# Decoder layer: a late head-norm part is chained behind the one before it, and the additions to finished tiles are spread over eight steps of one down-projection stage

## The chip, the core and the metric

The kernel is one program on one core of a Trainium2 chip. The core has five engines that run side by side, each with its own queue of instructions in a fixed order: TensorE (PE, matmuls), VectorE (DVE), ScalarE (ACT), GpSimd (POOL), and SyncE (SP), which here only issues DMAs. An instruction waits in its queue until the semaphores it names are reached; everything behind it on that engine waits with it. The metric is the time of one execution in microseconds (us), and the median over several is compared.

## What is computed

One layer of a hybrid decoder on 1024 tokens of width 1024, in float32:

```python
h = rms_norm(x, norm1_g);  proj = h @ w_in
y_a = rwkv7_branch(...)          # 8 heads x 64, a recurrence over time
y_b = stick_breaking_branch(...) # causal attention, 8 heads x 64
y_m = memory_branch(...)         # cross attention to 256 memory tokens
x = x + sum_b(sigmoid(G_b) * (y_b @ w_branch[b])) @ w_out
x = x + conv_ffn(x)              # up, causal conv of width 3, SwiGLU, down
# at the end of rwkv7_branch, for each token and head:
y = (y - mean(y)) * rsqrt(var(y) + 64e-5) * lnx_g + lnx_b   # then + bonus, * gate
```

## The kernel before

Every large matmul is done as three products of a high and a low half (`xhi`, `xlo`, `wh`, `wl` and the like): ScalarE copies the high half (L83), POOL subtracts to get the low half (L89), and both come from a weight tile that SP loaded.

**The recurrence** (`stage2`) runs over 16 chunks of 64 tokens, `c` = 0 to 15. A chunk has three parts, each ended by a `yield`: small matmuls into four PSUM tiles `g` and four VectorE copies (L656); matmuls with the inverse and ScalarE copies (L664); then matmuls for state and output, VectorE's state update (L674) and ScalarE's copies of the output into `self.y[p]` (L676), where p = 0 to 3 are pairs of heads. Between the parts, `weave` lets a list of filler items advance: gate items (`gate_item`: a projection in two PSUM tiles `mm`, ScalarE copies L885, a VectorE product with the row norms L886, ScalarE L889) and branch items (`branch_item`: a product in two tiles `mm` that VectorE multiplies by the gate, L1297, and adds, L1299). PSUM holds four tiles of tag `mm`; each item takes two, so the second item after an item takes its two back.

**The head norm** (`norm_part(g0, g1)`) works on output groups g0 to g1 - 1, of two chunks each. It is a generator: VectorE sums per head (L699) and one scaling (L700); ScalarE squares with a running sum (L706), four at a step; VectorE prepares (L192) and POOL takes the power (L195); two or three empty steps; then VectorE scales the heads (L715) in two steps. `stage2` advances it by one step after each `yield`. The parts are (0, 2), (2, 4), (4, 6), (6, 7) and (7, 8), started after chunks 3, 7, 11, 13 and 15. After the last chunk three more steps are taken, and `group_norm` takes the rest while it turns the heads by transposes (L122), multiplies by the gain (L729), adds (L730), and splits into high (L734) and low (L735) halves. `branch_last` then multiplies those by the last branch's weights: the gate of each output tile (L1354), the sum of the branches (L1359), high and low copies (L1365, L1366).

**Order.** Instructions passed through `pinned` keep the order in which the program emits them on their engine; in `stage2` and `group_norm` (`strict`) each is also tied behind the one pinned before. The rest (such as L89, L195, L729, L885) is placed by a list scheduler.

**The down projection** (`down_phase`) has seven stages i = 1, 3, 6, 5, 7, 4, 2 of 11 steps f = 0 to 10. A step is 12 matmuls. `prep`, three steps ahead, loads an activation block and a weight block (L1843, L1846), forms the weight of stages 4 and 7 on VectorE (L1848), makes high halves on ScalarE (L1853, L1854) and low ones on VectorE (L1855) and POOL (L1856). `drain` at f = 10 empties the PSUM tiles and lists finished output tiles in `sums`, with the residual tile `x` that SP loads and the terms to add. In the next stage `complete(tt)` does the additions of tile tt at step tt (L1876), and `release` at f = 5 issues the stores on ScalarE's queue (L1873). After stage 7 there are two terms, `q` and `U`, so in stage 4 two additions a step. At step 9 of stage 4 `last_residual` reloads `q` (L1917) and adds it to `p1` (L1918).

Of the kernel before, what the change touches and what calls it, by code (L numbers as in the profile page):

```python
# [50 lines left out]
class Trunk:  # L51
# [549 lines left out]
    def stage2(self):  # L601
        nc = self.nc
        self.y = [self.t4("qk") for _ in range(4)]
        uv = self.t4("ys", n=512).rearrange("p (u c) -> p u c", u=8)
        U, v1s = [uv[:, p] for p in range(4)], [uv[:, 4 + p] for p in range(4)]
        nc.gpsimd.memset(uv[:, 0:4], 0.0)
        hq = [slice(0, 64), slice(64, 128)]
        heads = [(p, h2) for p in range(4) for h2 in range(2)]
        A, Y, W, S = (slice(o, o + 64) for o in range(0, 256, 64))
        Ls, VTs = {}, {}  # L610
        norm = iter(())

        def load(g, p, what="LV"):
            if "L" in what:
                last = (g * 4 + p) % 8 == 7
                Ls[g, p] = self.t4("it", n=1080)[:, :1024] if last else self.t4("at")
                nc.sync.dma_start(Ls[g, p], self.scr[p, g])
            if "V" in what and p % 2 == 0:
                V2 = self.t4("qk")
                for h2 in range(2):  # L620
                    nc.sync.dma_start(V2[hq[h2], h2 * 256 : h2 * 256 + 256], self.vd[p // 2, h2, g].rearrange("s c i -> s (c i)"))
                nc.sync.dma_start(V2[:, 512:768], self.td[p // 2, g].rearrange("h s p i -> (h s) (p i)"))
                for i in range(2):
                    VTs[g, p + i] = [V2[:, h2 * 256 + i * 128 : h2 * 256 + i * 128 + 128] for h2 in range(2)], V2[:, 512 + i * 128 : 640 + i * 128]

        for p in range(4):
            load(0, p, "L")
        yield
        for p in range(0, 4, 2):
            load(0, p, "V")  # L630
        yield
        for p in range(4):
            load(1, p)
        yield
        for c in range(NC):
            g, cc = c // 2, c % 2
            us = []
            for p in range(4):
                L, (V, TT) = Ls[g, p], VTs[g, p]
                us.append((  # L640
                    U[p], L[:, cc * 128 : (cc + 1) * 128], L[:, 256 + cc * 128 : 256 + (cc + 1) * 128],
                    L[:, 512 + cc * 256 : 512 + (cc + 1) * 256], [v[:, cc * 64 : (cc + 1) * 64] for v in V],
                    TT[:, cc * 64 : (cc + 1) * 64], v1s[p], self.ps("g")))

            def state(o, rs):
                for p, h2 in heads if c else ():
                    Up, ra, _, _, _, _, _, pb = us[p]
                    q = hq[h2]
                    self.mmul(pb[q, o], ra[q, rs], Up[q], start=True, stop=False)

            state(A, Y)
            for p, h2 in heads:
                _, _, _, M, wv, _, v1, pb = us[p]
                self.mmul(pb[hq[h2], A], M[hq[h2], h2 * 128 + 64 : h2 * 128 + 128], wv[h2][hq[h2]], start=(c == 0), stop=True)
                if h2 == 1:
                    self.pinned(nc.vector.tensor_copy(v1, pb[:, A]))  # L656
            yield
            next(norm, None)
            for p, h2 in heads:
                _, _, _, _, wv, tt, v1, pb = us[p]  # L660
                self.mmul(pb[hq[1 - h2], W], tt[hq[h2]], v1[hq[h2]], start=True, stop=True)
                if h2 == 1:
                    for q, w in zip(hq, wv[::-1]):
                        self.pinned(nc.scalar.activation(w[q], pb[q, W], AF.Copy))  # L664
            yield
            next(norm, None)
            state(Y, A)
            for p, (Up, ra, bt, M, wv, tt, v1, pb) in enumerate(us):
                for h2, q in enumerate(hq):
                    self.mmul(pb[q, Y], M[:, h2 * 128 : h2 * 128 + 64], wv[h2], start=(c == 0), stop=True)  # L670
                if c < NC - 1:
                    for h2, q in enumerate(hq):
                        self.mmul(pb[q, S], bt[:, q], wv[h2], start=True, stop=True)
                    self.pinned(nc.vector.scalar_tensor_tensor(Up, Up, self.pc[p][:, c : c + 1], pb[:, S], ALU.mult, ALU.add))  # L674
                for h2, q in enumerate(hq):
                    self.pinned(nc.scalar.activation(self.y[p][cc * 64 : cc * 64 + 64, g * 128 + h2 * 64 : g * 128 + h2 * 64 + 64], pb[q, Y], AF.Copy))  # L676
            if cc and g + 2 < NG:
                for p in range(4):
                    load(g + 2, p)
            yield  # L680
            next(norm, None)
            if c in (3, 7, 11, 13, 15):
                for _ in norm:
                    pass
                norm = self.norm_part(*{3: (0, 2), 7: (2, 4), 11: (4, 6), 13: (6, 7), 15: (7, 8)}[c])
                next(norm)
            if c == 13:
                self.gs = [self.load_gg(p) for p in range(2)]
        for _ in range(3):
            next(norm)  # L690
        self.norm = norm
# [1124 lines left out]
    def down_phase(self):  # L1816
# [58 lines left out]
        puts, sums = [], []  # L1875
        add = lambda o, a, b, op=ALU.add: self.pinned(nc.vector.tensor_tensor(o, a, b, op))  # L1876

        def complete(tt):
            for half, n, x, terms in sums:
                for y in terms:  # L1880
                    add(x[tt], x[tt], y[tt])
                puts.append((half, n, tt, x[tt]))
            if tt == 3:
                sums.clear()

        def release():
            for args in puts:
                put(*args)
            puts.clear()
# [36 lines left out]
        for s, (i, f) in enumerate(steps):  # L1926
# [10 lines left out]
                t_sums(s // 2)  # L1937
            if s + ahead < len(steps):
                prep(s + ahead)
            if f < 4:  # L1940
                complete(f)
            elif f == 5:
                release()
            if s in (2, 4):
                self.last_sums.pop(0)()
# [184 lines left out]
```

## Time and profile before

| | |
|---|---|
| median of 3 runs | 1786.35 us (1785.88 to 1787.78) |
| profiled execution, its own time | 1786.78 us |
| its span, first to last instruction | 1785.0 us |
| recurrence, chunk 13 to the last output copy of chunk 15 | about 942 to 983 us of the span |
| `group_norm` | about 983 to 1011 us |
| `branch_last` | from 1011.6 us |
| down phase, stage 4 | about 1720 to 1750 us |

A row of the profile gives start and length in us, the engine, the line of the kernel, the operation, the tiles (out<-in, numbers left out), shapes and count, and in brackets how long the engine had been idle before it and what ended that. PE rows overlap a little: a matmul of 512 columns follows the one before by 0.23 us.

### The profile page before, as it was taken

How to read it: one execution, taken by the hardware profiler on the slowest of the kernel's cores; microseconds unless marked ns; L12 is line 12 of the kernel's file. 1: busy time of each engine (PE TensorE's matmuls, PEld its weight loads, DVE VectorE, ACT ScalarE, POOL GpSimd, SP SyncE). 2: the span in 40 equal slices, each digit the busy share in tenths (PEclk: the TensorE clock that was granted, in tenths of full speed). 3: DMA queues.
4: the chain of work that ended last, by engine and by line, in shares of the span. 5: the costliest groups of instructions: out<-in, count | busy, mean ns of one | idle time of the engine just before them, and what ended most of it. 6: DMA issues, size and time to landing. Idle time of an engine off the chain costs nothing.

```text
span 1785.0 us, 27451 instructions
## 1 busy us (share of the span) xinstructions
PE 1775.7 (99%) x10481; PEld 1442.9 (81%) x10481; DVE 1184.1 (66%) x1687; ACT 882.8 (49%) x1667; POOL 697.1 (39%) x409
## 2 busy tenths in 40 slices
PE   9999999999999999999999999999999999999999
PEld 7777778878888888787777888888888888888887
DVE  5666674787888655243533882697767777795596
ACT  6543344466566635444556434454444445444343
POOL 1232252322221012022333322257777677545454
PEclk9999999999999999999999999999999999999999
DMA  4256574111112343658764662323323333396475
GB/s 185 72 167 188 180 247 152 51 56 43 54 57 69 111 126 93 201 181 280 264 229 146 236 210 98 115 89 124 101 89 110 109 109 113 109 330 219 142 248 200
DMA packets 120758, 263.39 MB, mean 148 GB/s; under 512 B 28330, under 2 KB 41130, under 8 KB 120499
## 3 DMA queue, kind: packets, MB, share of 16 engines
q1 hardware_dynamic: 82434, 193.31, 32.9%
q10 hardware_dynamic: 34416, 55.72, 8.5%
q0 software_dynamic: 3776, 12.62, 2.4%
q8 instruction: 82, 1.34, 0.3%
q14 instruction: 50, 0.40, 0.1%
HBM read 180.04 MB, written 81.53 MB: 147 GB/s over the span
## 4 chain that ended last, share of the span: by engine, by line
PE 62%; issue 1%; POOL 1%; ACT 1%; DVE 1%; DMA 0%; ACTq 0%; DVEq 0%; POOLq 0%; SPq 0%
PE mm L139 53%; PE g L139 8%; PE g L122 1%; POOL dw L1856 1%; DVE qk L715 0%; ACT wh L83 0%; DMA qk<-vd 0%; ACT w L885 0%; DVE w L886 0%; DVE keep L1876 0%; POOL l L1555 0%; ACT qk L664 0%; ACT ys L1020 0%; DVE wl L86 0%; ACT qk L1059 0%
## 5 line engine op out<-in xcount | busy, mean ns | idle before, releaser
L89 POOL TENSOR_TENSOR wl<-wr,wh 128x1024 fp32r<-128x1024 f32 x58 | 148.0, 2552 | 368.2 <-ACT wh L83 360.5
L139 PE MATMUL mm<-xhi,wh 128*128 128x512 f32 x784 | 260.6, 413 | 0.5 <-ACT w L936 0.4
L139 PE MATMUL mm<-xlo,wh 128*128 128x512 f32 x784 | 243.5, 392 | 0.7 <-DVE xlo L225 0.6
L139 PE MATMUL mm<-xhi,wl 128*128 128x512 f32 x784 | 242.2, 390 | 0.0
L139 PEld LDWEIGHTS mm<-xlo,wh 128*128 128x128 f32 x784 | 147.0, 188 | 34.0 <-DVE xlo L225 1.6
L139 PEld LDWEIGHTS mm<-xhi,wl 128*128 128x128 f32 x784 | 147.1, 188 | 32.6
L139 PEld LDWEIGHTS mm<-xhi,wh 128*128 128x128 f32 x784 | 136.5, 189 | 30.4 <-issue 7.9
L139 PE MATMUL mm<-dw,da 128*128 128x512 f32 x528 | 121.1, 390 | 0.0
L83 ACT ACTIVATE wh<-wr 128x1024 fp32r<-128x1024 f32 x75 | 79.5, 1060 | 81.0 <-PE mm L139 61.9
L139 PE MATMUL mm<-BT,l 128*128 128x512 f32 x504 | 118.0, 389 | 0.3 <-POOL l L1555 0.3
L139 PEld LDWEIGHTS mm<-dw,da 128*128 128x128 f32 x528 | 98.9, 188 | 21.7 <-DVE da L1855 1.2
L1856 POOL TENSOR_TENSOR dw<-draw,dw 128x512 fp32r<-128x512 f32 x55 | 83.1, 1520 | 77.0 <-ACT dw L1854 74.2
L985 DVE TENSOR_TENSOR_SCAN at<-at,at 128x128 f32<-128x128 f32 (+3 forms) x64 | 91.0, 1429 | 33.1 <-ACT at L979 33.0
L139 PEld LDWEIGHTS mm<-BT,l 128*128 128x128 f32 x504 | 94.5, 188 | 20.3 <-POOL l L1555 0.7
L139 PE MATMUL mm<-BT,wh 128*128 128x512 f32 x352 | 108.5, 389 | 0.1
L139 PE MATMUL mm<-B,wh 128*128 128x512 f32 x352 | 108.4, 389 | 0.0
L195 POOL TENSOR_TENSOR hf<-rs,half 128x16 f32<-128x16 f32 (+1 forms) x18 | 49.2, 2732 | 143.4 <-DVE rs L192 138.9
L1855 DVE TENSOR_TENSOR da<-draw,da 128x512 fp32r<-128x512 f32 x77 | 66.6, 873 | 49.0 <-ACT da L1853 48.6
L139 PE MATMUL g<-dw,da 128*128 128x512 f32 x396 | 90.5, 389 | 0.4 <-POOL dw L1856 0.4
L1853 ACT ACTIVATE da<-draw 128x512 fp32r<-128x512 f32 x77 | 48.3, 628 | 81.0 <-PE mm L139 31.7
L139 PEld LDWEIGHTS g<-dw,da 128*128 128x128 f32 x396 | 74.2, 188 | 16.2 <-POOL dw L1856 0.8
L1627 ACT ACTIVATE g<-u,params 128x512 f32<-128x512 f32 x88 | 65.2, 770 | 32.1 <-DVE u L1717 22.9
(345 smaller groups left out, 3956.6 us busy)
## 6 DMA issues: line engine op xcount, KB each, us to landing
wr<-in_w_in_dram SPq DMA_DIRECT2D x49, 512.0 KB, 3.8
draw<-actd SPq DMA_DIRECT2D x77, 256.0 KB, 3.1
at<-scr SPq DMA_DIRECT2D x28, 512.0 KB, 5.5
draw<-in_w_down_dram SPq DMA_DIRECT2D x55, 256.0 KB, 4.6
rw<-in_w_up_dram SPq DMA_DIRECT2D x22, 512.0 KB, 3.5
actd<-gall ACTq DMA_DIRECT2D x41, 256.0 KB, 3.1
gsd<-w ACTq DMA_DIRECT2D x20, 512.0 KB, 2.8
wr<-in_w_up_dram SPq DMA_DIRECT2D x18, 512.0 KB, 3.6
```

The lines of the kernel that those rows point to most:

```text
L83: ins = self.nc.scalar.activation(hi, raw, AF.Copy)
L89: self.last_wl = self.nc.gpsimd.tensor_tensor(lo, raw, hi.bitcast(F32), ALU.subtract)
L122: self.pinned(self.nc.tensor.transpose(out, in_, self.ident[:n, :n]))
L139: self.pinned(self.nc.tensor.matmul(*a, **k))
L195: nc.gpsimd.tensor_tensor(out, t[:, :n], self.half[:, :n], ALU.pow)
L985: self.pinned(nc.vector.tensor_tensor_scan(sn[:, :W][:, ::-1], sn[:, :W][:, ::-1], self.smask[:, 1024 - W :][:, ::-1], 1.0, ALU.mult, ALU. ...
L1627: keep(nc.scalar.activation(c, u[:, 2 + h * 512 : 514 + h * 512], AF.Identity, scale=self.par("cw2", m), bias=self.par("cb", m)))
L1853: self.pinned(nc.scalar.activation(A[:, 0], a, AF.Copy))
L1855: self.pinned(nc.vector.tensor_tensor(A[:, 1], a, A[:, 0].bitcast(F32), ALU.subtract))
L1856: nc.gpsimd.tensor_tensor(Wt[:, 1], w, Wt[:, 0].bitcast(F32), ALU.subtract)
```

## The change

Two edits, with no instruction added or removed.

In `stage2`, after chunk 13 the part (4, 6) is no longer run to its end there, and the part (6, 7) no longer starts there. The two are joined by `itertools.chain`, so (6, 7) starts when (4, 6) has been stepped to its end; what is left after chunk 15 is run through before (7, 8) starts.

In `down_phase`, in stage 4, `complete` takes one term a step over steps 0 to 7 instead of two a step over steps 0 to 3, and the stores are released at step 8 instead of step 5.

```diff
             next(norm, None)
-            if c in (3, 7, 11, 13, 15):
+            if c in (3, 7, 11, 15):
                 for _ in norm:
                     pass
-                norm = self.norm_part(*{3: (0, 2), 7: (2, 4), 11: (4, 6), 13: (6, 7), 15: (7, 8)}[c])
+                norm = self.norm_part(*{3: (0, 2), 7: (2, 4), 11: (4, 6), 15: (7, 8)}[c])
                 next(norm)
+            elif c == 13:
+                norm = itertools.chain(norm, self.norm_part(6, 7))
...
-        def complete(tt):
+        def complete(tt, part=None):
             for half, n, x, terms in sums:
-                for y in terms:
-                    add(x[tt], x[tt], y[tt])
-                puts.append((half, n, tt, x[tt]))
-            if tt == 3:
+                for j, y in enumerate(terms):
+                    if part in (None, j):
+                        add(x[tt], x[tt], y[tt])
+                if part != 0:
+                    puts.append((half, n, tt, x[tt]))
+            if tt == 3 and part != 0:
                 sums.clear()
...
-            if f < 4:
+            if i == 4 and f < 8:
+                complete(f // 2, f % 2)
+            elif i != 4 and f < 4:
                 complete(f)
-            elif f == 5:
+            elif f == (8 if i == 4 else 5):
                 release()
```

The new lines shift the numbers of later lines by two in the changed program: L699 becomes L701, L715 L717, L1297 L1299, and so on to L1876, which becomes L1878.

PE's order is the same in both programs. VectorE, at the end of the recurrence, before: `hn` and `hf` with 9071 and 9222 belong to the part (6, 7), those with 9353 and 9376 to (7, 8); `qk` 6786 to 6789 are the four output tiles; `w_1528` is the gate of a branch item.

```order
L886 TENSOR_TENSOR w_1528_9314<-w_1528_9314,rbc 128x1024
L715 TENSOR_SCALAR qk_6786<-qk_6786,hn_9071,hf_9222 128x64 x2
L715 TENSOR_SCALAR qk_6787<-qk_6787,hn_9071,hf_9222 128x64 x2
L715 TENSOR_SCALAR qk_6788<-qk_6788,hn_9071,hf_9222 128x64 x2
L715 TENSOR_SCALAR qk_6789<-qk_6789,hn_9071,hf_9222 128x64 x2
L699 TENSOR_REDUCE hn_9353<-qk_6786 128x2
L699 TENSOR_REDUCE hn_9353<-qk_6787 128x2
L699 TENSOR_REDUCE hn_9353<-qk_6788 128x2
L699 TENSOR_REDUCE hn_9353<-qk_6789 128x2
L700 TENSOR_SCALAR hn_9353<-hn_9353 128x8
L729 TENSOR_TENSOR at_9078<-g_9402,at_9078 128x512
L729 TENSOR_TENSOR at_9082<-g_9409,at_9082 128x512
```

The same place in the changed program, where (6, 7) has `hn` 9263 and 9264 and `hf` 9341, and the gate is `w_1518`:

```order
L888 TENSOR_TENSOR w_1518_9294<-w_1518_9294,rbc 128x1024
L731 TENSOR_TENSOR at_9055<-g_9402,at_9055 128x512
L731 TENSOR_TENSOR at_9059<-g_9409,at_9059 128x512
L192 TENSOR_SCALAR rs_9342<-hn_9264 128x8
L717 TENSOR_SCALAR qk_6786<-qk_6786,hn_9263,hf_9341 128x64 x2
L717 TENSOR_SCALAR qk_6787<-qk_6787,hn_9263,hf_9341 128x64 x2
L717 TENSOR_SCALAR qk_6788<-qk_6788,hn_9263,hf_9341 128x64 x2
L717 TENSOR_SCALAR qk_6789<-qk_6789,hn_9263,hf_9341 128x64 x2
L701 TENSOR_REDUCE hn_9353<-qk_6786 128x2
L701 TENSOR_REDUCE hn_9353<-qk_6787 128x2
L701 TENSOR_REDUCE hn_9353<-qk_6788 128x2
L701 TENSOR_REDUCE hn_9353<-qk_6789 128x2
```

The preparation of (6, 7), L192, which stood in chunk 14, now stands here, with the wait for POOL's power behind it. In both programs L192 of (7, 8), two L730, four scalings and the branch item's two products (L1297, now L1299) follow; the four L729 that stood between and behind them now all stand ahead of that L192. On POOL the power of (6, 7) stood ahead of two weight splits L89, and now stands behind them.

ScalarE at the same place, before, behind the last gate copy L889:

```order
L889 ACTIVATE w_1528_9314<-w_1528_9314 128x1024
L706 ACTIVATE jk_9360,hn_9354<-qk_6786,hn_9353 128x64
L706 ACTIVATE jk_9362,hn_9354<-qk_6786,hn_9353 128x64
L83 ACTIVATE wh_9426<-wr_9424 128x1024
L706 ACTIVATE jk_9364,hn_9354<-qk_6787,hn_9353 128x64
```

and now:

```order
L891 ACTIVATE w_1518_9294<-w_1518_9294 128x1024
L708 ACTIVATE jk_9325,hn_9264<-qk_6786,hn_9263 128x64
L708 ACTIVATE jk_9327,hn_9264<-qk_6786,hn_9263 128x64
L708 ACTIVATE jk_9329,hn_9264<-qk_6787,hn_9263 128x64
L708 ACTIVATE jk_9331,hn_9264<-qk_6787,hn_9263 128x64
L708 ACTIVATE jk_9333,hn_9264<-qk_6788,hn_9263 128x64
L708 ACTIVATE jk_9335,hn_9264<-qk_6788,hn_9263 128x64
L83 ACTIVATE wh_9426<-wr_9424 128x1024
L708 ACTIVATE jk_9337,hn_9264<-qk_6789,hn_9263 128x64
L708 ACTIVATE jk_9339,hn_9264<-qk_6789,hn_9263 128x64
L708 ACTIVATE jk_9360,hn_9354<-qk_6786,hn_9353 128x64
```

Eight squares of (6, 7) stand where those of (7, 8) began, and the weight copy L83 stands behind six of them instead of two.

ScalarE in `branch_last`, before; `mg` are copies of output tiles (9624 the first, 9634 the second), and `wh_9817` is the high half of the branch weight that the fifth output tile uses, with low half `wl_9818`:

```order
L1365 ACTIVATE mg_0_1_0_9618<-at_9624 128x256
L83 ACTIVATE at_9799<-wr_9801 128x1024
L83 ACTIVATE wh_9817<-wr_9815 128x1024
L1365 ACTIVATE mg_0_0_9608<-at_9634 128x512
L1365 ACTIVATE mg_0_0_0_9616<-at_9634 128x256
L1365 ACTIVATE mg_0_1_0_9618<-at_9634 128x256
```

and now:

```order
L83 ACTIVATE qk_9753<-wr_9755 128x1024
L1367 ACTIVATE mg_0_0_9608<-at_9634 128x512
L1367 ACTIVATE mg_0_0_0_9616<-at_9634 128x256
L1367 ACTIVATE mg_0_1_0_9618<-at_9634 128x256
L83 ACTIVATE at_9799<-wr_9801 128x1024
L83 ACTIVATE wh_9817<-wr_9815 128x1024
```

Both weight copies moved from ahead of the second tile's three copies to behind them.

## The prediction

> **What bounds the kernel now.** I read the page's engine rows first, then the chain that ended last, then PE's waits.
>
> ```profile
> PE 1775.7 (99%) x10481; PEld 1442.9 (81%) x10481; DVE 1184.1 (66%) x1687; ACT 882.8 (49%) x1667; POOL 697.1 (39%) x409
> PE 62%; issue 1%; POOL 1%; ACT 1%; DVE 1%; DMA 0%; ACTq 0%; DVEq 0%; POOLq 0%; SPq 0%
> PE g L139 <- DVE ys L656: 0.5, 1, 0.5
> PE g L139 <- POOL dw L1856: 0.4, 1, 0.4
> ```
>
> TensorE is busy for 99% of the span and heads the chain; all waits that the view puts down to its matmuls add up to 5.0 us (1.5 + 0.6 + 0.6 + 0.5 + 0.5 + 0.4 + 0.4 + 0.3 + 0.2). So an edit that leaves the matmuls alone can gain little, and any new wait of PE is paid in full. The two waits quoted lie where the two edits are. The timeline shows both, with VectorE's work ahead of the first:
>
> ```profile
> 958.66 3.65 DVE L715 TENSOR_SCALAR qk<-qk,hn,hf 128x64 f32<-128x64 f32 x16
> 962.23 0.86 DVE L699 TENSOR_REDUCE hn<-qk 128x2 f32<-128x128 f32 x4
> 963.48 0.72 PE L139 MATMUL g<-ys,qk 64*64 64x64 f32 x16 [0.46 <-DVE ys L656]
> 1740.08 10.95 PE L139 MATMUL g<-dw,da 128*128 128x512 f32 x47 [0.36 <-POOL dw L1856]
> ```
>
> **What the edits remove.** At the end of chunk 13 VectorE did 16 scalings and 4 sums in one block, 4.4 us, ahead of the copy that chunk 14's matmul needed. The block goes: PE gains 0.46. In the down phase one addition a step in place of two lets the weight splits start earlier; the 0.36 may go. Together 0.82 us, and no other wait of PE stands near either edit.
>
> **What the first edit moves.** The part (6, 7) took its 8 squares and its power during chunk 14. Now they stand behind chunk 15, so two norm parts, each sums, squares, power, scalings, follow one another at the end, and the pinned order holds VectorE in that row. What stands behind them there:
>
> ```profile
> 983.67 1.06 ACT L889 ACTIVATE w<-w 128x1024 f32<-128x1024 f32 x1 [0.57 <-DVE w L886]
> 986.50 0.35 ACT L706 ACTIVATE jk<-qk,hn 128x64 f32<-128x64 f32 x1 [1.77 <-DVE hn L700]
> 986.98 0.35 ACT L706 ACTIVATE jk<-qk,hn 128x64 f32<-128x64 f32 x1
> 987.33 1.04 ACT L83 ACTIVATE wh<-wr 128x1024 fp32r<-128x1024 f32 x1
> 988.45 2.38 POOL L89 TENSOR_TENSOR wl<-wr,wh 128x1024 fp32r<-128x1024 f32 x1 [5.89 <-ACT wh L83]
> 969.33 1.67 POOL L195 TENSOR_TENSOR hf<-rs,half 128x8 f32<-128x8 f32 x1 [0.89 <-DVE rs L192]
> 991.35 2.01 POOL L195 TENSOR_TENSOR hf<-rs,half 128x8 f32<-128x8 f32 x1 [0.52 <-DVE rs L192]
> 983.56 1.87 DVE L715 TENSOR_SCALAR qk<-qk,hn,hf 128x64 f32<-128x64 f32 x8
> 986.24 0.17 DVE L700 TENSOR_SCALAR hn<-hn 128x8 f32<-128x8 f32 x1
> 993.40 0.98 DVE L715 TENSOR_SCALAR qk<-qk,hn,hf 128x64 f32<-128x64 f32 x4 [0.92 <-POOL hf L195]
> 994.29 1.28 DVE L1297 TENSOR_TENSOR w<-mm,w 128x512 f32<-128x512 f32 x2
> 998.81 0.61 PE L139 MATMUL mm<-xhi,wh 128*128 128x512 f32 x2
> ```
>
> The last two rows are the place that decides. L1297 empties the two `mm` banks of the last branch item. There are four such banks, each item takes two, one gate item follows, and the second gate item, which starts at 998.81, takes those two back. L1297's halves end at about 994.95 and at 995.57, so the first bank has 3.8 us in hand.
>
> Now the new row, on the trace's clock. ScalarE is done with L889 at 984.73. Six squares at 0.48 (986.98 less 986.50): 987.61. L83 1.04: 988.65. Two squares: 989.6. VectorE's 0.17: 989.8. POOL's split of that weight runs 988.7 to 991.1 and stands ahead of the power, so the power of (6, 7) (1.67) ends at 992.8, and VectorE waits 3 us for it. Eight scalings, four sums and L700 took 983.56 to 986.41, 2.85, and one PSUM product L729 of 0.65 now stands among them: 996.3. Eight squares of (7, 8) at 0.48: 1000.2. L192 and the power (0.2 and 2.01): 1002.45; the adds L730 lie beside it. Four scalings (993.40 to 994.29, 0.89), then L1297: its halves, 0.6 apart, end at 1004.05 and 1004.65, 9.1 later. PE waits from 998.81 to 1004.1, 5.3, and its second matmul, 0.23 on, 0.4 more for the second bank: **+5.7**. The ends: if squares or power overlap better by a microsecond, 4.7; with hand-overs of up to 0.1 that I left out (L83 ends at 988.37, the split starts at 988.45), 5.9. The transposes at 1001.54 that need the new scalings come after this wait and are covered by it.
>
> **The second wait.** Behind the gate item PE reads the second half of the normed heads:
>
> ```profile
> 1014.32 1.07 PE L139 MATMUL mm<-qk,wh 128*128 128x512 f32 x4
> 1014.13 0.63 ACT L734 ACTIVATE qk<-qk 128x512 fp32r<-128x512 f32 x1 [2.71 <-DVE qk L730]
> 1002.48 2.67 DVE L886 TENSOR_TENSOR w<-w,rbc 128x1024 f32<-128x1024 f32 x1 [0.67 <-ACT w L885]
> 996.09 1.22 DVE L1299 TENSOR_TENSOR w<-w,w 128x1024 f32<-128x1024 f32 x1
> 1001.42 2.64 POOL L89 TENSOR_TENSOR wl<-wr,wh 128x1024 fp32r<-128x1024 f32 x1 [3.20 <-ACT wh L83]
> ```
>
> The fourth of these matmuls (1015.0) needs the copy that ended at 1014.76: 0.24 in hand. VectorE got from L1297 (995.57) to that copy in 19.2, of which 0.67 was waiting, and one L729 of 0.6 now stands ahead of L1297: 17.9, so 1022.5. PE, 5.7 late, is there at 1020.7: **+1.8**. Two things shift this. L886 ended 1.09 after POOL's split did, and L1299 of the same size took 1.22: VectorE sat out the split. The split will lie under the add L730 now (+1.2) and no longer under L886 (-1.45). The ends are 0.6 and 2.2.
>
> **The third wait.** The next branch weight is split later, since ScalarE's two high copies L83 now stand behind three copies L1365 of the second output tile, which wait for VectorE's L1359:
>
> ```profile
> 1024.31 3.56 DVE L1366 TENSOR_TENSOR mg<-at,mg 128x512 fp32r<-128x512 f32 x3
> 1027.79 3.49 DVE L1359 TENSOR_TENSOR at<-at,w 128x512 f32<-128x512 f32 x2
> 1028.10 2.63 POOL L89 TENSOR_TENSOR wl<-wr,wh 128x1024 fp32r<-128x1024 f32 x1 [0.51 <-ACT wh L83]
> 1034.29 0.61 PE L139 MATMUL mm<-qk,wl 128*128 128x512 f32 x2
> 1000.52 1.29 DVE L735 TENSOR_TENSOR A<-qk,qk 128x512 fp32r<-128x512 f32 x2
> ```
>
> It was ready at 1030.73 for 1034.29, and is wanted at 1041.8 now. With L1359 done at 1031.28 and VectorE some 6.3 late: 1037.6, two small copies 0.8, two L83 of 1.04, two splits of 2.63 from 1039.5 on: 1044.7, a wait of 2.9. But L1359 and L1366 had sat out splits: two such operations alone took 1.29 (L735), so 2.2 of each row may not recur. The wait is 0 to 2.9; I take **+0.6**, since one of the two excesses is enough to end most of it.
>
> The Trainium skill speaks to this price ("SBUF — State Buffer", section "Who interferes with whom"): a VectorE instruction with both inputs in SBUF and a GpSimd one that reads SBUF shut each other out for a whole instruction, whichever came first. By the copied rows the third wait is 2.9; by that rule, with the splits moved, it all but goes. The trace agrees where it shows such a pair (L886 above); no row of it shows the moved splits, so I kept both ends.
>
> **The second edit.** It adds no instruction: eight additions stay eight, and `q` is still read by step 6, ahead of its reload in step 9. What moves is the release of the four stores, from step 5 to step 8:
>
> ```profile
> 1739.00 0.82 ACTq L1873 DMA_DIRECT2D out_dram<-it  x2
> 1741.85 0.63 ACT L1853 ACTIVATE da<-draw 128x512 fp32r<-128x512 f32 x1 [2.25 <-DMA out_dram<-it]
> 1749.19 5.78 DVE L1918 TENSOR_TENSOR keep<-keep 128x512 f32<-128x512 f32 x4
> 1754.89 0.68 DVE L1855 TENSOR_TENSOR da<-draw,da 128x512 fp32r<-128x512 f32 x1
> 1750.86 9.50 PE L139 MATMUL mm<-dw,da 128*128 128x512 f32 x40
> ```
>
> They held ScalarE's next copy for 2.25. SP's residual loads into the same tiles, issued after step 10, wait for those stores too, with `actd` loads queued behind them; they had five steps for it and now have two, and a step is 12 x 0.227 = 2.72. The nearest need is the split done at 1755.57: the last stage's third step starts at 1750.86 + 24 x 0.227 = 1756.30 and reads it two matmuls later, 1756.76, 1.2 in hand. If all 2.25 land on it PE waits 1.05; if none, 0. I take **+0.3**.
>
> **Sum.** 5.7 + 1.8 + 0.6 + 0.3 - 0.46 - 0.36 = +7.6. The profiled execution took 1786.78 around a span of 1785.0, 0.43 above the median 1786.35. So 1794.4 as that execution, **1793.9** against the median. A measurement here can tell about 0.2%, 3.6 us.
>
> **Rivals.** *The cover holds* (not slower): L1297 comes less than 3.8 late, PE waits nowhere, and the two gains stay: -0.82, 1785.5. It decides at 998.8 on VectorE. For it: 3.8 is much, and a matmul's bank is inferred from the pool, not from a record. Against: three waits in a row (3 for the first power, 4 for squares, 2 for the second power) would have to lose 5.3. Chance 0.05.
>
> *The third wait stays whole*: the splits meet VectorE again, +2.3 on the sum: 1796.2. For it: the rows copied as they are. Chance 0.13.
>
> *A cold array*: after the long pause PE runs slow for a while. The start of the trace shows it:
>
> ```profile
> 1.46 5.66 PE L139 MATMUL g<-qk 128*128 128x512 f32 x13 [1.46 <-DVE qk L202]
> ```
>
> These 13 matmuls took 0.435 each, against 0.23 later (10.95 for 47): 2.7 lost. The same after 5.3 us of pause would cost 2.7, of which the second wait hides 1.8: +0.9, up to +2.7 if that wait is gone: 1794.8 to 1796.6. The longest wait in the trace is 1.5, so no row shows a pause that long. Chance 0.10. The Trainium skill ("TensorE: Matmul & The Clock Gate", "What's actually happening") has the array halve its clock after an idle window of about 3.4 us and return after as much work, which here may or may not fit into the pause.
>
> The forecast has 0.68; 0.04 is left for what I don't see, half of it slower. **Range**: the low end is 4.7 + 0.6 - 0.8, +4.5, 1790.9; the high end takes 5.9 + 2.2 + 2.9 + 1.1 without the second gain, about +11.7, and a little of the clock: 1798.5. Slower by over 0.2%: 0.68 + 0.13 + 0.10 + 0.02 = 0.93; within: 0.05 + 0.01 = 0.06; faster: 0.01.
>
> **What would show it.** Right: no wait at the start of chunk 14's last products; VectorE idle before the first scaling of (6, 7) by about 3 for POOL and before the second L192 by about 3 for ScalarE; a PE wait of 5 to 6 on VectorE's branch product at the second gate item; one of 1 to 2 on ScalarE's copy some 17 us later. Wrong: that matmul without a wait, or a new wait of PE over 1 us anywhere ahead of 960 or in the down phase.

## The result, and the profile after

The changed kernel took **1803.81 us** (median of five runs, 1801.01 to 1805.54) beside 1787.04 for the kernel before: ratio 1.0094, 95% interval 1.0080 to 1.0109, 16.8 us slower. Five further runs gave 1801.19 beside 1786.93, ratio 1.0081 (1.0067 to 1.0094), 14.3 slower. The forecast, 1793.9 with a range up to 1798.5, had the sign and about half of the size; the result lies above the range. The profiled execution took 1801.01 around a span of 1799.2, 14.2 more than the span before.

First the page of the changed kernel (engine rows, chain by engine), then its list of PE's waits:

```profile
PE 1779.1 (99%) x10481; PEld 1444.5 (80%) x10481; DVE 1184.0 (66%) x1687; ACT 882.7 (49%) x1667; POOL 694.5 (39%) x409
PE 58%; issue 2%; POOL 2%; DVE 2%; ACT 1%; DMA 1%; ACTq 0%; SPq 0%; DVEq 0%; POOLq 0%
PE mm L139 <- DVE w L1299: 7.1, 1, 7.1
PE mm L139 <- DVE da L1857: 3.0, 1, 3.0
PE mm L139 <- POOL wl L89: 0.5, 1, 0.5
PE mm L139 <- DVE at L1356: 0.4, 1, 0.4
```

The two waits that the change was to remove (`ys` L656, `dw` L1856) are gone from the list, and the four above are new. (A wait of 0.8 on L222 at 7.3 us is left out: one of up to 1.1 comes and goes there from kernel to kernel, also in one below that has neither edit.) PE is busy for 3.4 us longer with the same 10,481 matmuls: some of them ran slower.

Since PE's order is the same in both kernels, each matmul can be held against itself. From start to start, the changed kernel differs from before at these places and at no others by more than 0.1 us behind the first 15 us:

| place (time in the changed kernel) | forecast | measured |
|---|---|---|
| first products of chunk 14 (962.8) | -0.46 | -0.53 |
| second gate item, banks of the branch item (1005.4) | +5.7 | +7.26 |
| the matmuls right behind it | not in the sum | +1.76 |
| `branch_last`, normed heads (second wait) | +1.8 | 0 |
| `branch_last`, weight split (third wait, 1043.3) | +0.6 | +0.80 |
| `branch_last` into `out_proj`, L1356 (1066.2) | not seen | +1.02 |
| stage 4 of the down phase (1749.7) | -0.36 | -0.63 |
| third step of the last stage (1769.5) | +0.3 | +3.32 |
| the matmuls right behind it | not in the sum | +1.53 less 0.25 |

The sum is +14.3; less 0.1 in the first 15 us it is the 14.2 of the span. (A short wait costs a little more than its row says: a matmul's modelled end lies 0.39 behind its start, the next one may start 0.23 behind it, and the first pairs after a stop are slower.)

The first wait, in the timelines of VectorE, GpSimd and PE of the changed kernel:

```profile
988.52 1.66 DVE L192 TENSOR_SCALAR rs<-hn 128x8 f32<-128x8 f32 x1 [1.15 <-ACT jk L708]
990.25 1.67 POOL L195 TENSOR_TENSOR hf<-rs,half 128x8 f32<-128x8 f32 x1
991.96 1.88 DVE L717 TENSOR_SCALAR qk<-qk,hn,hf 128x64 f32<-128x64 f32 x8 [1.79 <-POOL hf L195]
999.17 0.17 DVE L192 TENSOR_SCALAR rs<-hn 128x8 f32<-128x8 f32 x1 [3.29 <-ACT jk L708]
999.42 2.01 POOL L195 TENSOR_TENSOR hf<-rs,half 128x8 f32<-128x8 f32 x1 [7.50 <-DVE rs L192]
1001.47 3.15 DVE L717 TENSOR_SCALAR qk<-qk,hn,hf 128x64 f32<-128x64 f32 x4 [0.92 <-POOL hf L195]
1002.23 2.34 POOL L89 TENSOR_TENSOR wl<-wr,wh 128x1024 fp32r<-128x1024 f32 x1 [0.80 <-ACT wh L83]
1004.54 1.27 DVE L1299 TENSOR_TENSOR w<-mm,w 128x512 f32<-128x512 f32 x2
1005.37 1.30 PE L139 MATMUL mm<-xhi,wh 128*128 128x512 f32 x2 [7.10 <-DVE w L1299]
1006.46 1.06 PE L139 MATMUL mm<-xlo,wh 128*128 128x512 f32 x2
```

This is the row that the prediction worked out: the first power, 8 scalings, 8 squares, the second power, 4 scalings, then L1299, and the matmul behind it. Two things are not in it. The four scalings took 3.15 instead of 0.98, and they lie over GpSimd's split L89: three of them took 0.31 or 0.32, and the last, begun at 1002.14, took 2.48 and ended at 1004.62, the split at 1004.57. And a pair of matmuls took 1.06, where such a pair takes 0.62 elsewhere.

The second is the clock. The view by windows, cut at the times at which the trace's clock records change (columns: length, busy time and count of PE, weight loads, VectorE, ScalarE, GpSimd, then the granted clock):

```profile
995.18:998.59 3.41, 3.09 (x14) 2.23 (x12) 0.70 (x3) 3.01 (x14) 0.00 (x0) 1.00 0.01 2
998.59:1002.00 3.41, 0.00 (x0) 0.00 (x0) 1.91 (x6) 2.55 (x6) 2.01 (x1) 1.00 0.00 0
1002.00:1005.42 3.42, 0.05 (x1) 0.08 (x1) 3.42 (x5) 0.15 (x1) 2.34 (x1) 0.50 0.00 0
1005.42:1008.83 3.41, 3.41 (x8) 2.61 (x9) 3.41 (x6) 1.76 (x4) 0.62 (x1) 0.50 0.43 154
1008.83:1012.24 3.41, 3.41 (x20) 2.84 (x20) 3.41 (x8) 0.59 (x1) 0.00 (x0) 1.00 0.37 154
```

The clock was halved in two stretches of 3.41. The first fell into the pause and cost nothing; in the second, PE was busy throughout with 8 matmuls.

In the last down stage, from the timelines of ScalarE's queue, VectorE, GpSimd and PE:

```profile
1757.88 1.63 ACTq L1875 DMA_DIRECT2D out_dram<-dx  x2
1759.61 0.63 ACT L1855 ACTIVATE da<-draw 128x512 fp32r<-128x512 f32 x1 [3.67 <-PE g L139]
1760.84 8.06 POOL L1858 TENSOR_TENSOR dw<-draw,dw 128x512 fp32r<-128x512 f32 x5 [2.62 <-ACT dw L1856]
1760.88 6.90 DVE L1922 TENSOR_TENSOR keep<-keep 128x512 f32<-128x512 f32 x4
1767.70 1.74 DVE L1857 TENSOR_TENSOR da<-draw,da 128x512 fp32r<-128x512 f32 x1
1769.50 5.77 PE L139 MATMUL mm<-dw,da 128*128 128x512 f32 x17 [3.05 <-DVE da L1857]
```

ScalarE stood still for 3.67 around the two last stores; VectorE's four additions to the kept tile came behind that and took 6.90; the split that PE needed came behind those. GpSimd's five splits, which wait for ScalarE's copies too, run in one piece beside them: each of the four additions and VectorE's split took 1.74 to 1.80. Before, three additions took 1.77 or 1.78 beside such splits, and the fourth and VectorE's split 0.68 each.

### The profile page after: what moved, and what is told of

It is laid out like the page before. It is cut to its first block, busy times and chain, and to the rows that moved or that the text cites. A ratio compares the mean times of both kernels' runs of the same rounds, so it can differ in the third digit from the quotient of the medians.

```text
span 1799.2 us, 27448 instructions
## 1 busy us (share of the span) xinstructions
PE 1779.1 (99%) x10481; PEld 1444.5 (80%) x10481; DVE 1184.0 (66%) x1687; ACT 882.7 (49%) x1667; POOL 694.5 (39%) x409
## 4 chain that ended last, share of the span: by engine, by line
PE 58%; issue 2%; POOL 2%; DVE 2%; ACT 1%; DMA 1%; ACTq 0%; SPq 0%; DVEq 0%; POOLq 0%
PE mm L139 50%; PE g L139 7%; POOL dw L1858 1%; PE g L122 1%; DMA wr<-in_w_out_dram 1%; ACT wh L83 0%; DVE w L888 0%; DMA draw<-actd 0%; DVE mg L1368 0%; DMA qk<-vd 0%; POOL hf L195 0%; DVE keep L1922 0%; DMA it<-x2d 0%; DVE qk L717 0%; ACT jk L708 0%
## 5 line engine op out<-in xcount | busy, mean ns | idle before, releaser
L89 POOL TENSOR_TENSOR wl<-wr,wh 128x1024 fp32r<-128x1024 f32 x58 | 146.6, 2528 | 367.7 <-ACT wh L83 356.3
L83 ACT ACTIVATE wh<-wr 128x1024 fp32r<-128x1024 f32 x75 | 79.5, 1060 | 80.8 <-PE mm L139 65.6
```

The lines of the kernel that those rows point to most:

```text
L83: ins = self.nc.scalar.activation(hi, raw, AF.Copy)
L89: self.last_wl = self.nc.gpsimd.tensor_tensor(lo, raw, hi.bitcast(F32), ALU.subtract)
```

## The experiments

Times are compared with runs of the kernel before that were made beside them: 1786.93 (20 runs) for `chain_only`, `down_only`, `late_release` and `after_again`; 1786.75 (15 runs) for `chain_later_split`, `chain_free_product`, `two_releases` and `side_by_side`; 1786.93 (14 runs) for the others.

**The two edits apart.** `chain_only` is before with the first edit alone, `down_only` before with the second alone.

> The first edit alone. In the changed kernel TensorE was 10.2 late from before at the first product of the output projection (of that 0.7 earned, 7.1 waited, 1.8 at half clock, the rest in two waits of about 0.5). If the two edits do not touch each other, this kernel is 10 slower than before: 1797. If the clock is what the second edit's place loses, because the first edit has used something up, this one alone is 12 or more slower. The third theory, that the chain itself costs what the prediction said and the rest is the second edit, gives 7.6 less 0.3 less -0.36, about 1794.5.

> The second edit alone. If the edits do not touch each other: 3.05 of waiting in the third step of the last stage and 1.7 at half clock, less 0.36 to 0.6 earned in stage 4, about 4.2 slower, 1791. If the wait there comes about only because the work ahead of it is 10 late (a DMA that meets other traffic), it is gone here, and the time is 0.4 faster than before.

Measured: `chain_only` 1798.51 (1796.09 to 1800.59), ratio 1.0063 (1.0051 to 1.0076), +11.6. `down_only` 1791.45 (ten runs, 1788.92 to 1792.58), ratio 1.0023 (1.0014 to 1.0032), +4.5. Together +16.1 beside the +14.3 to +16.8 of both, so within the scatter they add up. They may still touch: the profile of `chain_only` has a wait of 0.8 at the third step of the last stage (1768.4), the place of the second edit's wait, though its down phase is that of before; `chain_later_split` and `chain_free_product` below do not have it. The first wait stands at 7.1 in `chain_only`, the last at 3.3 in `down_only`. But in the profile of `down_only` this wait, longer than in the changed kernel, is followed by matmuls at full speed:

```profile
1750.33 6.05 PE L139 MATMUL mm<-dw,da 128*128 128x512 f32 x26
1759.65 6.69 PE L139 MATMUL mm<-dw,da 128*128 128x512 f32 x27 [3.27 <-DVE da L1855]
```

27 of them took 6.69, where 26 ahead of the wait took 6.05. What decides that is taken up below.

**Late stores or spread additions.** `late_release` keeps before's two additions a step and only releases the stores later:

```diff
-            elif f == 5:
+            elif f == (8 if i == 4 else 5):
                 release()
```

> Before, with one thing changed: the four stores of stage 4 are released at step 8 in place of step 5; the additions stay two a step over steps 0 to 3. Theory A, the late stores: ScalarE's queue stands still behind them (3.7 in the changed kernel, 2.25 before), two to three steps ahead of the last stage, and the wait of about 3 at its third step is here too, with the slow matmuls behind it: 3 to 5 slower than before. Theory B, the spread: single additions at steps 4 to 7 push VectorE's splits together with the four additions to the kept tile, and the stores matter little: no wait over 0.5 here, same time as before.

Measured: 1790.8 (11 runs, 1787.83 to 1794.34), ratio 1.0021 (1.0013 to 1.0030). ScalarE, VectorE and PE in its timelines:

```profile
1750.43 0.63 ACT L1853 ACTIVATE da<-draw 128x512 fp32r<-128x512 f32 x1 [4.43 <-PE g L139]
1751.71 6.89 DVE L1918 TENSOR_TENSOR keep<-keep 128x512 f32<-128x512 f32 x4
1758.52 1.78 DVE L1855 TENSOR_TENSOR da<-draw,da 128x512 fp32r<-128x512 f32 x1
1760.36 10.00 PE L139 MATMUL mm<-dw,da 128*128 128x512 f32 x30 [2.67 <-DVE da L1855]
```

The same row with the additions as before: the late stores do it (theory A). `two_releases` is the counter-test, the additions spread and `complete` written as in the change, but three of the four stores at step 5 and the last at step 8:

```diff
-            if f < 4:
+            if i == 4 and f < 8:
+                complete(f // 2, f % 2)
+            elif i != 4 and f < 4:
                 complete(f)
-            elif f == 5:
+            if f == 5 or (i, f) == (4, 8):
                 release()
```

> The second edit alone, additions one a step over eight steps, but the three tiles that are finished by step 5 are released at step 5, and only the fourth store waits for step 8. By the theory of the late stores, most of the 3.3 of waiting in the third step of the last stage goes: 0 to 1 slower than before, and the 0.4 of stage 4 are earned: 1786.5 to 1788. By the theory of the spread additions the 3 stay: 1790 to 1791.

Measured: 1786.07 (11 runs, 1785.61 to 1787.93), ratio 0.9996 (0.9987 to 1.0005). VectorE's row is back to the shape of before:

```profile
1747.97 5.78 DVE L1920 TENSOR_TENSOR keep<-keep 128x512 f32<-128x512 f32 x4
1753.68 0.68 DVE L1855 TENSOR_TENSOR da<-draw,da 128x512 fp32r<-128x512 f32 x1
```

No wait in the last stage is left, and the wait of 0.36 in stage 4 is gone. So the spread costs nothing, and the release costs all of it.

**The scalings beside the split.** `chain_later_split` is the first edit alone, with the high copy of the weight of the first `branch_last` tile tied on ScalarE behind the copy of the third head pair (`self.third`), so that GpSimd's split starts later:

```diff
+                self.last_fin = self.third if d == 0 else None
                 w = self.split_w(self.I["w_br"][0, d // 2])
+                self.last_fin = None
```

> The first edit alone, with the high copy of the weight of the first branch_last tile moved on ScalarE's queue behind the copy of the third head pair, so that GpSimd's split of it starts some 4 later. In the changed kernel four scalings of the part (7, 8) took 3.15 in place of 0.98 while that split ran. If the split held VectorE, they take about 0.9 here and the wait at the second gate item falls from 7.1 to 4.9; the split then meets other VectorE work and gives part of the 2.2 back as a wait further on: between 0 and 2.2 faster than the first edit alone, 1796.3 to 1798.5. If the scalings were late for a reason of their own (the power, the squares), 3.15 and 7.1 stay.

Measured: 1798.32 (1797.79 to 1798.65), as slow as the first edit alone. Its timelines of VectorE, ScalarE and PE:

```profile
1001.48 0.98 DVE L717 TENSOR_SCALAR qk<-qk,hn,hf 128x64 f32<-128x64 f32 x4 [0.92 <-POOL hf L195]
1006.51 2.39 DVE L717 TENSOR_SCALAR qk<-qk,hn,hf 128x64 f32<-128x64 f32 x1
1003.20 1.30 PE L139 MATMUL mm<-xhi,wh 128*128 128x512 f32 x2 [4.93 <-DVE w L1301]
1036.88 1.06 ACT L83 ACTIVATE at<-wr 128x1024 fp32r<-128x1024 f32 x1 [2.68 <-DMA wr<-in_w_out_dram]
1043.07 0.73 PE L139 MATMUL mm<-qk,wl 128*128 128x512 f32 x2 [1.87 <-POOL wl L89]
```

The four scalings are at 0.98 and the wait at 4.93, as expected of a split that held them. Moved, it holds one scaling of the second set instead (2.39 for one that takes 0.3 alone), and the third wait rises from 0.5 to 1.87, with slow matmuls behind it: all was given back. That third wait ends at 1043.07, and in `chain_only` at 1042.89: PE came earlier, but the two splits that it waits for did not, because ScalarE's copy ahead of them waits for a load of an output weight (the L83 row; 1036.65 in `chain_only`). By the Trainium skill ("SBUF — State Buffer", "Who interferes with whom") a `tensor_scalar` can enter a mode in which it and GpSimd shut each other out; these two places agree with that.

**The branch product out of the row.** `chain_free_product` is the first edit alone, with the two products L1299 of the last branch item not pinned; the scheduler then puts them right behind L888, ahead of the scalings of (6, 7).

```diff
-            self.pinned(nc.vector.tensor_tensor(g[:, hs], pp[h], g[:, hs], ALU.mult))
+            ins = nc.vector.tensor_tensor(g[:, hs], pp[h], g[:, hs], ALU.mult)
+            if (b, d) != (2, 7):
+                self.pinned(ins)
```

> The first edit alone, but the two products that empty the banks of the last branch item are not pinned, and the scheduler places them ahead of the scalings of the part (6, 7), 11 earlier. If the first wait is there only because those products stand in VectorE's fixed row behind two norm parts, the 7.1 are gone. The norm parts are still as late, and the next that needs them is late instead: the transposes of the second half at about 1002 (1 to 2 of waiting, by the last scalings), and the fourth pass of the first branch_last tile (up to 4). Sum 3 to 6 slower than before, 1790 to 1793, and with no single pause of 3 or more, few slow matmuls. If something else held TensorE at the gate item, the 7.1 stay.

Measured: 1796.08 (1795.15 to 1798.48), ratio 1.0054 (1.0041 to 1.0066), +9.3. In its list of waits:

```profile
PE g L122 <- DVE qk L717: 3.3, 1, 3.3
PE mm L139 <- POOL wl L89: 2.3, 1, 2.3
```

The wait at the gate item is gone, so it was the place of L1299 in the row. The norm is late all the same: the transposes wait 3.3 for the last scalings, the third wait is 2.3, and both are followed by slow matmuls. I had put the sum at 3 to 6: the transposes wait longer than the 1 to 2 that I expected, the third wait was not in it, and I had counted on few slow matmuls.

**(6, 7) at its old time, beside (4, 6).** `side_by_side` does not drain (4, 6) after chunk 13, but starts (6, 7) there as before and steps both through chunk 14; the down phase is that of `two_releases`:

```diff
+            next(late, None)
-            if c in (3, 7, 11, 13, 15):
-                for _ in norm:
+            if c in (3, 7, 11, 15):
+                for _ in itertools.chain(norm, late):
                     pass
...
+            elif c == 13:
+                late = self.norm_part(6, 7)
+                next(late)
```

> The part (4, 6) is not run to its end after chunk 13, as in the change, but (6, 7) is started there all the same, and the two are stepped side by side through chunk 14, the second with tiles hm of its own; the down phase as in two_releases. If what costs is that (6, 7) comes late, and not that (4, 6) is spread, the squares and power of (6, 7) are done in chunk 14 as before, no wait over 0.7 comes near 960 to 1050, and TensorE gains 0.5 at chunk 14. With two_releases' own loss, 0.5 less than that kernel: 1786 to 1787.5. If the spread scalings themselves hold VectorE up, waits come back at the first products of chunks 14 and 15.

Measured: 1803.15 (four runs, 1802.75 to 1803.81), 16 slower, and no new wait of PE behind the first 15 us. Instead its matmuls are slower from the first stages on (PE's sum is 1792.9, with a granted clock of 1.00). The two extra tiles `hm` of 64 bytes had pushed all tiles of two pools behind them by 128 bytes. `side_by_side_same_place` takes these tiles from the tag `hf`, and no other tile moves:

```diff
-        nm, vs = [self.small("hm" if g0 == 6 else "hn", [128, 16]) for _ in range(2)]
+        nm, vs = [self.small("hf", [128, 16], bufs=4) if g0 == 6 else self.small("hn", [128, 16]) for _ in range(2)]
```

> side_by_side once more with the same order on every engine; only the two small tiles of (6, 7) now come from the tag hf, so that no tile of the kernel lies elsewhere than before. In side_by_side two tiles of 64 bytes had moved every later tile of two pools by 128 bytes, and TensorE's matmuls on these tiles followed one another by 0.231 in place of 0.227 from the start of the program on. If the place of the tiles does that, all matmuls take 0.227 here, the 16 of loss go, and what is left is two_releases less 0.5: 1785 to 1786.5. If the loss comes from the side-by-side stepping or its waits, 1803 stays.

Measured: 1785.62 (11 runs, 1784.82 to 1786.05), ratio 0.9992 (0.9983 to 1.0001). Rows of the groups by line, of `side_by_side` and then of `side_by_side_same_place` (busy sum, mean ns of one):

```profile
L139 PE MATMUL mm<-B,wh 128*128 128x512 f32 x352 | 110.4, 395 | 0.0
L139 PE MATMUL mm<-dw,da 128*128 128x512 f32 x528 | 121.2, 390 | 0.0
```

```profile
L139 PE MATMUL mm<-B,wh 128*128 128x512 f32 x352 | 108.4, 389 | 0.0
L139 PE MATMUL mm<-dw,da 128*128 128x512 f32 x528 | 121.2, 390 | 0.0
```

Slow are those matmuls whose tiles had moved; `dw` and `da` lie in a pool that stayed. Which of a matmul's two operands does it was not separated. With the place restored, neither the chunk-14 wait nor any other remains in this part: what costs in the first edit is that (6, 7) comes late, not that (4, 6) is spread. This version is the fastest of all, 1.3 below before, and still within what can be told from no change.

**The clock.** `pauses_wide` and `pauses_near` are before with spare scalings behind VectorE's first copy of seven chunks, so that PE pauses there:

```diff
                     self.pinned(nc.vector.tensor_copy(v1, pb[:, A]))
+                    for _ in range({4: 27, 5: 18, 6: 36, 8: 21, 9: 30, 10: 24, 12: 44}.get(c, 0) if p == 0 else 0):
+                        self.pinned(nc.vector.tensor_scalar(pz, pz, 1.0, None, ALU.mult))
```

> Before, with a number of scalings of a spare 128x64 tile put behind VectorE's first copy of chunks 4, 5, 6, 8, 9, 10 and 12 (27, 18, 36, 21, 30, 24 and 44 of them, 0.23 each), so that TensorE pauses seven times, by about 1 to 7, each time at the same place of a chunk. If the clock halves once a pause is longer than a fixed length, the matmuls behind every pause above that length take twice as long for about 3.5, and behind none below it. If it is decided by when the pause falls, pauses of 2.5 to 3.5 go either way and only the long ones always cost it. Either way a slow stretch costs 1.7 to 1.8, whatever the length of the pause.

> The same with 23, 25, 27, 24, 26, 28 and 22 scalings, seven pauses of about 2.2 to 3.6 that stand close together. Fixed length: one bound parts the pauses with a slow stretch from those without. Decided by when the pause falls: longer ones without and shorter ones with it, as the 3.3 without and the 2.7 with it in the last down stage of two earlier kernels already suggest.

Measured, one run each: the pauses came out at 1.3 to 11.5 and 2.4 to 6.5, longer than I meant. The clock records of all profiles here change only at multiples of 3.41 (3.41, 6.83, 10.24, 13.65, 23.89, 27.31, ...), at a place of the program that differs from run to run. I took each such stretch of sixteen profiles, and in it the time in which PE was idle. Behind a stretch at full clock: idle up to 1.70, full again in every case; 1.73 to 1.92, two halved and four full; 1.95 and more, halved in all 26. Behind a halved stretch it stayed halved for idle times from 0.57 up (20 cases) and was full again at 0.44 and below (28 cases). So a pause is judged by what falls into one stretch. Two windows of `down_only`, between which the 3.27 was divided, and the same of `late_release`, where 2.04 of its 2.67 fell into one:

```profile
1754.88:1758.30 3.42, 1.50 (x7) 0.92 (x5) 3.42 (x3) 1.15 (x2) 3.42 (x3) 1.00 0.79 245
1758.30:1761.71 3.41, 2.06 (x9) 1.72 (x10) 3.41 (x5) 0.00 (x0) 0.75 (x1) 1.00 0.30 106
```

```profile
1756.31:1759.72 3.41, 1.37 (x7) 0.79 (x5) 3.41 (x3) 1.15 (x2) 2.96 (x3) 1.00 0.81 247
1759.72:1763.13 3.41, 2.77 (x7) 2.19 (x8) 3.41 (x6) 0.00 (x0) 0.04 (x1) 0.50 0.52 159
```

Neither theory was whole: there is a bound, but on the idle time inside a stretch, so for a pause it comes out as chance between about 1.7 and 3.8 (twice 1.92, divided evenly between two stretches).

**The spread of the changed kernel.** Four more profiles of it.

> The changed kernel once more, for a second profile. Its five times lay between 1801.0 and 1805.5 and its granted clock between 0.994 and 0.997, so the time of one run is not the time of the next. If the losses are the two waits of TensorE seen in the first profile (7.1 at the second gate item, 3.05 in the last down stage) and the slow matmuls behind each (8 and 10 of them at 0.43 in place of 0.23: 1.8 and 1.7), the second profile shows the same two waits, within 0.5, and a slower run has more or longer slow stretches behind waits that are about as long. If the waits themselves vary by microseconds, the cause is something that these two profiles will show to differ ahead of the wait, a DMA above all.

> The changed kernel, a third profile. Its ten times so far go from 1800.3 to 1805.5, its granted clock from 0.998 to 0.994. If the clock is granted anew every 3.41, and halved for the next 3.41 where TensorE stood still for more than about 1.9 of the last, each halved stretch is 0.00095 of the mean clock: 0.997 are three, 0.994 are six. Then the time of a run goes by how the grid lies over the same waits: about 1.5 for each halved stretch that falls on work. A slower run would show the same waits of 7.1 and 3 and more halved stretches. If the waits differ from run to run, the slower one has waits that are not in the first two profiles.

> As after_third, a fourth profile: the grid lies otherwise over the program. 7.1 of waiting always covers one whole stretch of 3.41, or nearly, so the gate item always meets at least one halved stretch; the wait of about 3 in the last stage may fall so that neither stretch has 1.9 of it (about one run in six), and this run is then some 1.5 shorter.

> As after_third, a fifth profile. It adds one more place of the grid: the theory of the grid expects the waits of 7.1 and 3 once more, within 0.5, and a time that goes with the number of halved stretches; the other theory expects a further wait in a slower run.

Measured: 1801.19 (five runs), and single runs of 1802.61, 1799.37 and 1800.81. The first wait is 7.1 in all five profiles. The last is 3.2, 3.6, 2.9 and 3.2; the 3.6 and the 2.9 were divided between two stretches and followed by full clock, the others not. And one wait does vary, the fourth at L1356: 0.3, 1.7, 0.4, 1.1 (0.4 in the first profile). So both theories hold in part: the grid, and a further wait. The third profile shows both, the longer fourth wait and a halved stretch behind it (clock 0.50 from 1067.62 to 1071.03):

```profile
PE mm L139 <- DVE da L1857: 3.6, 1, 3.6
PE mm L139 <- DVE at L1356: 1.7, 1, 1.7
```

One halved stretch is 0.00095 of the mean clock (half of 3.41 in 1800). The ten runs of `down_only` sort by it: two at 1.000, 1788.92 and 1789.82; three at 0.999, 1790.48 to 1791.35; five at 0.998, 1791.56 to 1792.58. The first five runs of the changed kernel had 0.997 to 0.994. No profile caught one of 0.994, so where its further halved stretches lie stays open.

## Why the prediction was right and wrong

The direction was right and the size was not: +14.3 in this profile where the sum had +7.6. Three terms were too small: the first wait (7.26 for 5.7), the second edit (3.32 for 0.3), and the slow matmuls behind these two pauses, which the sum put at nothing (1.76 and 1.28). One wait was not seen (1.02), and one that stood at 1.8 did not come.

**The two gains** were right: -0.46 and -0.36 became -0.53 and -0.63.

**The first wait** was right in its row and place. Up to the second power the real row was 1.0 earlier than mine (it ended at 1001.43, I had 1002.45). What was mis-sized is the next item, "four scalings (993.40 to 994.29, 0.89)": they took 3.15. I had moved the split of that weight in my arithmetic for the second wait, to under the add L730, and not asked what else it would lie on; it lay on the scalings. That is +2.2, shown by `chain_later_split`. PE's own gain made it arrive 0.7 earlier, and the step cost 7.26 in place of 5.7. The place itself is shown by `chain_free_product`: with the products moved, the wait is gone.

**The clock** is the step that was left out of the sum: the rival of the cold array, given a chance of 0.10 because "no row shows a pause that long", came true, and at two places. The slow rows at the start of the trace were the evidence, and I read the bound as a long pause. The runs show that 1.95 of idle time within a stretch of 3.41 is enough. The Trainium skill ("TensorE: Matmul & The Clock Gate", "What's actually happening") has a free-running window of 3413 ns, and the records agree; its condition of an idle window of about 3.4 us does not, since stretches that were idle for 1.95 to 2.9 halved the clock here as well. A wait of 5.3 and more covers at least 1.95 of some stretch wherever the grid lies, so the slow matmuls belonged into the sum: +1.76 at the first wait and, by the grid, +1.53 at the last.

**The second wait** did not come. The copy was done at about 1021.6 (I had 1022.5): VectorE took 15.8 to it from the end of the branch product, where I had 17.9. And PE was held up by 2.6 more than I had added and came later still. In `chain_later_split`, where the first wait is shorter, 0.4 of it is there. That the longer first wait would cover it was said of the cold array, and is how it went.

**The third wait** came out in size, 0.5 for +0.6 and 0 to 0.5 in all five profiles, but not by the row that I had worked out, so the size is luck. From the views of VectorE, ScalarE and GpSimd, with ScalarE's copy of before as the last row:

```profile
1033.25 1.29 DVE L1361 TENSOR_TENSOR at<-at,w 128x512 f32<-128x512 f32 x2
1036.94 1.06 ACT L83 ACTIVATE at<-wr 128x1024 fp32r<-128x1024 f32 x1 [1.64 <-DMA wr<-in_w_out_dram]
1038.09 2.62 POOL L89 TENSOR_TENSOR at<-wr,at 128x1024 fp32r<-128x1024 f32 x1 [6.44 <-ACT at L83]
1040.66 2.57 POOL L89 TENSOR_TENSOR wl<-wr,wh 128x1024 fp32r<-128x1024 f32 x1
```

```profile
1023.86 1.05 ACT L83 ACTIVATE at<-wr 128x1024 fp32r<-128x1024 f32 x1
```

Both excesses were gone, as I had argued for one: L1361 took 1.29 for 3.49, and L1368 ahead of it 1.35 for 3.56. But ScalarE's copy then waited for a load that stands in no term of mine. SP issued it at 1029.26, 11.1 later than before (1018.21), behind a weight copy of ScalarE, and it took 7.66 for 5.26. Without that wait of 1.64 the splits would have been in time (an estimate from these rows; no run took it alone). The same load holds the splits where the first wait is shortened or gone, and the third is then 1.9 and 2.3.

**The fourth wait**, L1356, was not seen. In the chain of the changed kernel it follows from a load of an output weight, 5.6 us long, behind which ScalarE's copies and then VectorE's stand. The load took 5.8 before, but SP now issues it at 1056.55, 10.6 later than before (1045.96), where PE is 9.1 late: 1.5 of its slack is gone. Ahead of the issue the chain has VectorE's L1368 of 1049.56, 5.34 long beside two splits (4.30 before). Where the wait is 1.7 the load took 6.5. No run tests this cause, and why the load's length varies was not tried.

**The second edit** is the term that failed by size: "If all 2.25 land on it PE waits 1.05". I took the hold that the stores had at step 5 for the most they could have at step 8. The hold was 3.67 to 4.43 there, and the wait is the sign of being wrong that the prediction had named, one of over 1 us in the down phase. VectorE's row L1922 started 2.15 later against PE than before, took 1.12 longer (6.90 for 5.78), and the split behind it 1.07 longer (1.74 for 0.68): 4.3 in all, and less the slack of 1.2 that I had right, it is 3.1. So half is the hold itself and half the rows that now lie beside GpSimd's splits, one more addition and VectorE's split; that half is read from the rows, no run took it alone. What the stores wait for is read from the program: each issue waits until an earlier DMA on the same semaphore has landed, and at step 8 these are loads that SP had issued 4 to 5 us before. The changed kernel's trace fits: the load of `keep` issued at 1754.06 landed at 1757.86, and the third store went at 1757.88; the weight load of 1754.49 landed at 1759.09, and the fourth went at 1759.17. That the late release is the cause is shown twice, by `late_release` and `two_releases`.

## What to carry to other kernels

When a change lets the tensor engine stand still, do not price only the wait: find how much idle time one stretch of the clock's grid can get (here 1.95 of 3.41 was enough), and add up to half a stretch for each pause that can reach it. When an operation moves in time, lay it over every row that it now meets, on all engines and on the queue that issues the loads, and not only over the one you were looking at. A bound for a moved DMA is not the stall it had at its old place: ask what its queue waits for at the new one.

## What the runs showed of the hardware that I had not expected

- The clock is granted in stretches of 3.41 us whose grid lies differently in each run; a run's time differs by about 1.5 us for each halved stretch that falls on work, which spreads the runs of a kernel with pauses of about 3 us over 3.7 us (`down_only`), while before spreads over 2.5.
- A shift of 128 bytes of the tiles that matmuls read cost 0.9% of the program: the same 900 matmuls took 207.83 in place of 204.31, 0.231 for 0.227 each. In the two kernels with pauses the same pools lay 256 bytes further, and these 900 took 204.0.
- A scaling of a 128x64 tile, 0.3 alone, took up to 2.48 beside one split on GpSimd, and ended with it (1004.62 and 1004.57).
